# A decoder layer in three-product fp32: four of eight k pairs of the gate/up chunks in seven products, and an adding DMA for four additions

## The chip, the cores and the metric

The kernel runs on one core of a Trainium2 chip. The metric is the device time of one execution in microseconds (us). The engines are TensorE (PE; its weight loads are PEld), VectorE (DVE), ScalarE (ACT), GpSimd (POOL) and SyncE (SP); each takes its own instructions strictly in order, and an instruction that waits holds up all that stand behind it on its engine.

## The reference

One decoder layer on x of 256 x 2048 floats: an input projection that feeds a retention branch and a sliding-window attention branch, an output projection, and a SwiGLU feed-forward with d_ff = 5632. The change is in the feed-forward, with a small part at the very start (the first columns of the input projection).

```python
proj = h @ w_in[l]
...
h = layer_norm(DEEPNORM_ALPHA * h + merged @ w_out[l], ln1_g[l], ln1_b[l])
ffn = (jax.nn.silu(h @ w_gate[l]) * (h @ w_up[l])) @ w_down[l]
h = layer_norm(DEEPNORM_ALPHA * h + ffn, ln2_g[l], ln2_b[l])
```

## The kernel before

**Products.** Every fp32 product is made of three products of a shorter float type: high x high, high x low (the low part is that of the weights) and low x high. So each block of weights that a DMA brings on SP's queue (1 MB, tile `raw`) is split: ACT casts it to the high part (`wh`, L304 or L217), and DVE subtracts that from the block to get the low part (`wl`, L305 or L218). There are three buffers for `wh` and three for `wl` (pool `spl`). One matmul has 128 x 128 operands on one side and 512 columns on the other.

**Chunks.** The work is a stream of chunks. A gate/up chunk (f = 1 to 10) computes 512 columns of the gate and the same 512 of the up projection for both halves of the 256 rows, so it has four sums C11, C12, C21, C22, over 16 k tiles taken as eight pairs. An ordinary pair ("s") needs 8 products of a k tile with a half of the columns, 24 matmuls. Some pairs are computed in seven products in place of eight, by Winograd's form of Strassen's method ("S" pairs). An S pair is worked in two steps: step R (9 matmuls, into the sums P1, C11 and C12; cast `wh` of 1536 columns), and step T (12 matmuls, into P5, P7, P6 and C21), whose weights are differences of the blocks (`tsum`, three DVE instructions, L290 to L292) that are cast into `th` (ACT, L304) and `tl` (DVE, L305). There is one buffer for `th` and one for `tl` (pool `sp2`). `pair_seq(n)` gives the order of the pairs: S, s, S, s, ... until n S pairs are done, then the s pairs that are left. With n = 3 (NQ before) a gate/up chunk has three S and five s pairs, 183 matmuls, and its last three pairs are s pairs.

**Ends.** After the last T step, `mids` joins P1, P5, P6 and P7 into four partial results (one ACT copy of P1, L734, and four DVE additions). At the end of a chunk `done_gu` adds C11, C12, C21 and C22 to them (DVE), applies silu (ACT) and multiplies (DVE). Eight transposes on PE (L540) and a split into high and low parts (`ph`, `pl`, by ACT and DVE) make the left operand of the down projection of it. The sums of a chunk lie in banks of PSUM, eight in all; the first steps of the next chunk need banks that ACT's copy or DVE's additions have read out.

**Order.** The gate/up chunks stand in three parts, f = 0 to 3, 4 to 7 and 8 to 10 (f = 0 is a plain chunk), and each part is followed by its down-projection chunks, which are pair chunks as well: two after each of the first two parts, and one, with two plain chunks, after the last. NS is the number of S pairs in these. Left operands of S pairs are sums of the k tiles' parts (`hsums`, `psums`: small DVE additions and a split). Small background jobs are mixed in, two steps after each step of a chunk (`pump`). A list scheduler then lays out the instructions of each engine, so that the final order is not that of the code.

## Time and profile before

| | us |
|---|---|
| median of 3 runs (1432.46 to 1432.58) | 1432.5 |
| the profiled execution | 1432.52 |
| its span, first to last instruction | 1430.7 |
| PE busy | 1423.1 (99%) |
| DVE busy | 1135.0 (79%) |
| ACT busy | 699.3 (49%) |

The span is what the trace covers; 1.8 us of the profiled execution lie around it. A busy time is the time in which an engine had at least one instruction under way. Durations of neighbouring matmuls overlap, so the time that one costs is the distance of two starts, not its duration; the same holds on ACT and DVE, by less.

### The profile page before, as it was taken

The page shows a single profiled execution, that of the slowest core. Times are in us where ns is not written, and L with a number is a line of the kernel's source. Part 1 is how long each engine was busy: PE and PEld are TensorE (multiplying, and loading weights), DVE is VectorE, ACT ScalarE, POOL GpSimd, SP SyncE. Part 2 cuts the span into 40 slices and gives each one's busy share as a digit, 9 for nine tenths or more (in the row PEclk, how much of TensorE's full clock was granted, in tenths as well). Part 3 has the DMA queues.
Part 4 walks back from the last instruction along what each step waited for, and adds up shares of the span by engine and source line. Part 5 has one row for each costly group of instructions (what it writes and reads, how often), then busy time and mean ns, then how long its engine had stood idle before and what let it go on. Part 6 is the DMA issues. An engine that isn't in the chain of part 4 may idle for free.

```text
span 1430.7 us, 16141 instructions
## 1 busy us (share of the span) xinstructions
PE 1423.1 (99%) x6494; PEld 1165.0 (81%) x6494; DVE 1135.0 (79%) x1271; ACT 699.3 (49%) x664; POOL 0.9 (0%) x6
## 2 busy tenths in 40 slices
PE   9999999999999999999999999999999999999998
PEld 6878888878888878788888888888888888888886
DVE  6764555487878879776589989888999988898986
ACT  5465444344445445444345555445555455455542
...
GB/s 327 222 158 118 143 115 122 150 174 210 198 209 166 210 188 206 206 244 272 160 177 177 208 184 211 193 209 193 196 195 206 206 206 181 197 211 200 213 234 88
DMA packets 40235, 274.75 MB, mean 192 GB/s; under 512 B 4704, under 2 KB 4832, under 8 KB 8160
## 3 DMA queue, kind: packets, MB, share of 16 engines
...
## 4 chain that ended last, share of the span: by engine, by line
PE 98%; DVE 1%; DMA 0%; ACT 0%; SPq 0%; issue 0%
PE bank L324 21%; PE bank L326 21%; PE bank L325 21%; PE acc L235 9%; PE acc L233 9%; PE acc L234 9%; PE tr L540 2%; PE mx L589 2%; PE mx L618 1%; PE bank L540 1%; PE bank L235 1%; PE bank L234 1%; PE bank L233 1%; DMA xraw<-in_xw 0%; PE bank L685 0%; PE mx L656 0%
## 5 line engine op out<-in xcount | busy, mean ns | idle before, releaser
L304 ACT CAST wh<-raw 128x2048 fp32r<-128x2048 f32 (+1 forms) x174 | 307.7, 1769 | 295.1 <-PE bank L326 223.8
L305 DVE TENSOR_TENSOR wl<-raw,wh 128x2048 fp32r<-128x2048 f32 (+1 forms) x174 | 366.4, 2108 | 62.0 <-ACT wh L304 61.6
L218 DVE TENSOR_TENSOR wl<-raw,wh 128x2048 fp32r<-128x2048 f32 x70 | 160.1, 2288 | 79.6 <-ACT wh L217 79.3
L217 ACT CAST wh<-raw 128x2048 fp32r<-128x2048 f32 x70 | 133.5, 1909 | 175.0 <-PE acc L235 110.8
L324 PE MATMUL bank<-wh,hh 128*128 128x512 f32 x460 | 179.6, 390 | 0.0
L326 PE MATMUL bank<-wh,hl 128*128 128x512 f32 x460 | 179.1, 389 | 0.0
L325 PE MATMUL bank<-wl,hh 128*128 128x512 f32 x460 | 179.0, 389 | 0.0
L305 DVE TENSOR_TENSOR tl<-tsum,th 128x2048 fp32r<-128x2048 f32 x58 | 132.6, 2287 | 34.2 <-ACT th L304 34.0
L304 ACT CAST th<-tsum 128x2048 fp32r<-128x2048 f32 x58 | 111.0, 1914 | 95.1 <-DVE tsum L292 78.0
L324 PE MATMUL bank<-wh,xh 128*128 128x512 f32 x364 | 144.5, 397 | 0.0
L326 PE MATMUL bank<-wh,xl 128*128 128x512 f32 x364 | 141.8, 389 | 0.0
L325 PE MATMUL bank<-wl,xh 128*128 128x512 f32 x364 | 141.7, 389 | 0.0
L233 PE MATMUL acc<-wh,xh 128*128 128x512 f32 x352 | 140.9, 401 | 0.4 <-ACT wh L217 0.3
L235 PE MATMUL acc<-wh,xl 128*128 128x512 f32 x352 | 138.7, 394 | 0.0
L234 PE MATMUL acc<-wl,xh 128*128 128x512 f32 x352 | 138.0, 392 | 0.7 <-DVE wl L218 0.7
L326 PEld LDWEIGHTS bank<-wh,hl 128*128 128x128 f32 x460 | 86.3, 188 | 18.0
L325 PEld LDWEIGHTS bank<-wl,hh 128*128 128x128 f32 x460 | 86.4, 188 | 17.8
L324 PEld LDWEIGHTS bank<-wh,hh 128*128 128x128 f32 x460 | 86.4, 188 | 17.7
L324 PE MATMUL bank<-wh,ph 128*128 128x512 f32 x220 | 85.9, 390 | 0.0
L325 PE MATMUL bank<-wl,ph 128*128 128x512 f32 x220 | 85.6, 389 | 0.0
L326 PE MATMUL bank<-wh,pl 128*128 128x512 f32 x220 | 85.1, 389 | 0.0
L324 PEld LDWEIGHTS bank<-wh,xh 128*128 128x128 f32 x364 | 68.3, 188 | 15.8 <-issue 1.4
(287 smaller groups left out, 2315.2 us busy)
## 6 DMA issues: line engine op xcount, KB each, us to landing
raw<-in_w_gu SPq DMA_DIRECT2D x88, 1024.0 KB, 4.9
raw<-in_w_ip SPq DMA_DIRECT2D x56, 1024.0 KB, 4.9
raw<-in_w_in SPq DMA_DIRECT2D x40, 1024.0 KB, 4.9
raw<-in_w_dp SPq DMA_DIRECT2D x38, 1024.0 KB, 4.9
raw<-in_w_out SPq DMA_DIRECT2D x16, 1024.0 KB, 5.3
raw<-in_w_dl SPq DMA_DIRECT2D x6, 1024.0 KB, 4.9
...
hres<-in_x SPq DMA_DIRECT2D x1, 2048.0 KB, 7.9
```

The source lines that it names most:

```text
L217: nc.scalar.copy(out=h[:, 0:m], in_=r)
L218: nc.vector.tensor_sub(out=l[:, 0:m], in0=r, in1=h[:, 0:m].bitcast(F32))
L233: nc.tensor.matmul(self.acc[t], lhsT=xh, rhs=wh[:, j], start=st, stop=False)
L234: nc.tensor.matmul(self.acc[t], lhsT=xh, rhs=wl[:, j], start=False, stop=False)
L235: nc.tensor.matmul(self.acc[t], lhsT=xl, rhs=wh[:, j], start=False, stop=sp)
L304: nc.scalar.copy(out=h_, in_=r)
L305: nc.vector.tensor_sub(out=l_, in0=r, in1=h_.bitcast(F32))
L324: nc.tensor.matmul(self.acc[p], lhsT=xh, rhs=wh[:, j], start=st, stop=False)
L325: nc.tensor.matmul(self.acc[p], lhsT=xh, rhs=wl[:, j], start=False, stop=False)
L326: nc.tensor.matmul(self.acc[p], lhsT=xl, rhs=wh[:, j], start=False, stop=sp)
L540: m = nc.tensor.transpose(ps[:, i], s, ident)
L589: nc.tensor.matmul(sps[u][:, i], lhsT=qT[u * HD:(u + 1) * HD, h // 2], rhs=kT[u * HD:(u + 1) * HD, g, 0:W], start=True, stop=True)
```

## The change

It has five parts.

1. NQ goes from 3 to 4: four of the eight pairs of each gate/up chunk are S pairs, and the order of the pairs is S, s, S, s, S, s, S, s. NS goes from (3, 3, 2) to (3, 3, 3): one more S pair in the last down-projection pair chunk. On PE this takes away 33 matmuls of 512 columns (three in each of ten gate/up chunks, three in the last pair chunk). For each of these 11 new S pairs ACT has one cast of 2048 columns (`th`) more and one of the `wh` casts of 1536 in place of 2048; DVE has `tl` (2048), and `tsum` (one of 1024 and two of 512) more, and one `wl` of 1536 in place of 2048. There is one more `hsums` step before the gate/up chunks and one more `psums` step in the last part.
2. In seven of the ten gate/up chunks (f = 1, 2, 4, 5, 6, 8, 9) the four additions of `done_gu` go: ACT copies C11, C21, C12 and C22 from PSUM into the tile `cc` (four copies of 512 columns), and one DMA on POOL's queue adds the four tiles of `mids` (1 MB, SBUF to SBUF) onto it. A job `swish` applies silu (ACT, one instruction of 1024 columns) and multiplies (DVE, one of 1024) twelve and more job steps later, and the transposes wait for it. In f = 3, 7 and 10, the last of each part, DVE still adds, and all background jobs are run out first (`drain`).
3. The four tiles of `mids` become one tile `q4`; the scratch tiles of `hsums` are taken from the `tsum` buffer; the `psums` job pauses 14 (or 6) job steps after each pair.
4. The first chunk's blocks of x and weights are 1, 1, 1, 1 and six times 2 k tiles in place of 1, 1 and seven times 2, six buffers in place of four, with up to five blocks under way; the fourth warm-up matmul, of 256 columns, goes; the constants come in two DMAs on ACT's queue instead of one.
5. Some small tiles move to other pools (attention's in the pool `sma`, the sums of the left operand in the pool `hq`).

```diff
--- before.py
+++ after.py
@@ -28,7 +28,7 @@
 NWARM = 3
 TD = 14
 CP = 1
-NQ = 3
+NQ = 4
 NX = 2
 PG = 4
 NGEN = 3
@@ -334,7 +334,7 @@
                 self.done(self)
 
     LOOK_B = 3
-    XB = 4
+    XB = 6
 
     class Stream:
         def __init__(self):
@@ -354,7 +354,7 @@
         def ahead(self):
             while True:
                 cb = self.casts[min(self.ci, len(self.casts) - 1)][2]
-                while self.bi < min(len(self.blocks), cb + LOOK_B):
+                while self.bi < min(len(self.blocks), cb + (LOOK_B if cb >= len(XS) - LOOK_B else XB - 1)):
                     ch, b = self.blocks[self.bi]
                     ch.dma(b)
                     self.bi += 1
...
@@ -434,10 +435,8 @@
     for i in range(NWARM):
         wp = bank("tr", [P, C])
         nc.tensor.matmul(wp, lhsT=warm[:, 0:P], rhs=warm[:, P:P + C], start=True, stop=True)
-    wp = bank("tr", [P, C])
-    nc.tensor.matmul(wp[:, 0:SEQ], lhsT=warm[:, 0:P], rhs=warm[:, P:P + SEQ], start=True, stop=True)
-
-    XS = [1, 1, 2, 2, 2, 2, 2, 2, 2]
+
+    XS = [1, 1, 1, 1, 2, 2, 2, 2, 2, 2]
     xraw = {}
 
     def x_dma(b):
@@ -446,7 +445,8 @@
         nc.sync.dma_start(out=r[:, 0:XS[b]], in_=a["xw"][:, k:k + XS[b]])
         xraw[b] = r
         if b == 2:
-            nc.scalar.dma_start(out=cst[:, 0:NC0], in_=a["consts"][:, 0:NC0])
+            nc.scalar.dma_start(out=cst, in_=a["consts"][:, 0:P])
+            nc.scalar.dma_start(out=freq, in_=a["consts"][:, P:NC0])
             xraw["pos"] = xa.tile([P, LINE], I32, name="posi")[:, 0:2]
             nc.scalar.dma_start(out=xraw["pos"], in_=a["pos"])
 
...
@@ -727,16 +727,15 @@
 
     def mids(ch):
         tp, acc = sc["tp"], ch.acc
-        s1 = tp.tile([P, C], F32, name="s1")
-        vx = tp.tile([P, C], F32, name="vx")
-        w = tp.tile([P, C], F32, name="w")
-        x5 = tp.tile([P, C], F32, name="x5")
+        q = tp.tile([P, 4, C], F32, name="q4")
+        s1, vx, w, x5 = [q[:, i] for i in range(4)]
         nc.scalar.copy(out=s1, in_=acc["P1"])
         nc.vector.tensor_add(out=vx, in0=s1, in1=acc["P6"])
         nc.vector.tensor_add(out=w, in0=vx, in1=acc["P5"])
         nc.vector.tensor_add(out=vx, in0=vx, in1=acc["P7"])
         nc.vector.tensor_add(out=x5, in0=vx, in1=acc["P5"])
         ev["t"] = (s1, vx, w, x5)
+        ev["q"] = q
 
     def done_va(ch, j):
         acc = ch.acc
@@ -901,13 +900,13 @@
     sgf = {}
     ujobs = []
     parts = ((0, 4), (4, 8), (8, 11))
-    NS = (3, 3, 2)
+    NS = (3, 3, 3)
     f0_of = {f: f0 for f0, f1 in parts for f in range(f0, f1)}
     ND = {f: n for (f0, f1), n in zip(parts, NS) for f in range(f0, f1)}
 
     def done_g(ch, t, c):
         if t == 0:
-            sgf[c] = sc["fp"].tile([P, 2, C], F32, name="sg2", bufs=1)
+            sgf[c] = sc["fp"].tile([P, 4, C], F32, name="cc", bufs=1)
         nc.scalar.activation(out=sgf[c][:, t], in_=ch.acc[t], func=AF.Silu)
 
     def done_u(ch, t, c):
@@ -959,14 +958,16 @@
     def lhs_s(kp, i):
         return sc["sh"][:, i, kp], sc["sl"][:, i, kp]
 
-    def psums(ph, pl, k0, n):
-        yield
-        yield from hsums(ph, pl, sc["psh"], sc["psl"], n, k0)
+    def psums(ph, pl, k0, n, gap):
+        for _ in hsums(ph, pl, sc["psh"], sc["psl"], n, k0):
+            for _ in range(gap):
+                yield
 
     def hsums(hh, hl, sh, sl_, n, k0=0):
         for kp in range(n):
-            h2 = sc["tp"].tile([P, 2, 2, P], F32, name="s1")
-            sm = sc["tp"].tile([P, 4, P], F32, name="vx")
+            ts = sc["tp"].tile([P, 4, C], F32, name="tsum")
+            h2 = ts[:, 0].rearrange("p (k t c) -> p k t c", k=2, t=2)
+            sm = ts[:, 1].rearrange("p (k c) -> p k c", k=4)
             ks = slice(2 * kp, 2 * kp + 2)
             nc.vector.tensor_add(out=h2.rearrange("p k t c -> p k (t c)"), in0=hh[:, ks].bitcast(F32), in1=hl[:, ks].bitcast(F32))
             nc.vector.tensor_add(out=sm[:, 0], in0=h2[:, 0, 1], in1=h2[:, 1, 1])
@@ -982,31 +983,47 @@
 
     def flush():
         if "u" in ev:
-            f, args = ev.pop("u")
-            queue_p(f, [Job(u_bg(*arg)) for arg in args])
+            f, args, deps = ev.pop("u")
+            queue_p(f, [Job(u_bg(*arg), deps) for arg in args])
 
     def queue_p(f, js):
         kp = 2 * (f - f0_of[f])
         n = min(2, ND[f] - kp)
         if n > 0:
-            jobs["ps", f] = Job(psums(*pTs[f], kp, n), js)
+            jobs["ps", f] = Job(psums(*pTs[f], kp, n, 14 if f < 8 else 6), js)
 
     def done_gu(ch, f):
         acc = ch.acc
         s1, vx, w, x5 = ev["t"]
-        sg = sc["fp"].tile([P, 2, C], F32, name="sg2", bufs=1)
+        cc = sc["fp"].tile([P, 4, C], F32, name="cc", bufs=1)
         pTs[f] = (sc["pp"].tile([P, 4, SEQ], F32R, name="ph"), sc["pp"].tile([P, 4, SEQ], F32R, name="pl"))
-        nc.vector.tensor_add(out=sg[:, 0], in0=s1, in1=acc["C11"])
-        nc.scalar.activation(out=sg[:, 0], in_=sg[:, 0], func=AF.Silu)
+        us = [(cc, t, *pTs[f]) for t in range(2)]
+        if f + 1 not in (4, 8, 11):
+            for i, nm in enumerate(("C11", "C21", "C12", "C22")):
+                nc.scalar.copy(out=cc[:, i], in_=acc[nm])
+            nc.gpsimd.dma_start(out=cc, in_=ev["q"], accum_op=ALU.add)
+            ev["u"] = f, us, [Job(swish(cc))]
+            return
+        nc.vector.tensor_add(out=cc[:, 0], in0=s1, in1=acc["C11"])
+        nc.scalar.activation(out=cc[:, 0], in_=cc[:, 0], func=AF.Silu)
         nc.vector.tensor_add(out=w, in0=w, in1=acc["C12"])
-        nc.vector.tensor_add(out=sg[:, 1], in0=vx, in1=acc["C21"])
-        nc.scalar.activation(out=sg[:, 1], in_=sg[:, 1], func=AF.Silu)
-        nc.vector.tensor_mul(out=sg[:, 0], in0=sg[:, 0], in1=w)
+        nc.vector.tensor_add(out=cc[:, 1], in0=vx, in1=acc["C21"])
+        nc.scalar.activation(out=cc[:, 1], in_=cc[:, 1], func=AF.Silu)
+        nc.vector.tensor_mul(out=cc[:, 0], in0=cc[:, 0], in1=w)
         nc.vector.tensor_add(out=x5, in0=x5, in1=acc["C22"])
-        nc.vector.tensor_mul(out=sg[:, 1], in0=sg[:, 1], in1=x5)
-        ev["u"] = f, [(sg, t, *pTs[f]) for t in range(2)]
-        if f + 1 in (4, 8, 11):
-            flush()
+        nc.vector.tensor_mul(out=cc[:, 1], in0=cc[:, 1], in1=x5)
+        drain()
+        ev["u"] = f, us, []
+        flush()
+
+    def swish(cc):
+        for _ in range(12):
+            yield
+        tc.keep_in_program_order(nc.scalar.activation(out=cc[:, 0:2], in_=cc[:, 0:2], func=AF.Silu))
+        yield
+        yield
+        nc.vector.tensor_mul(out=cc[:, 0:2], in0=cc[:, 0:2], in1=cc[:, 2:4])
+        yield
 
     seq = pair_seq(NQ)
     for part, (f0, f1) in enumerate(parts):
...
-    sc["sh"] = hp.tile([P, 4, NQ, P], F32R, name="sh")
-    sc["sl"] = hp.tile([P, 4, NQ, P], F32R, name="sl")
...
+    hq = ppc.enter_context(tc.tile_pool(name="hq", bufs=1, side=RIGHT))
+    sc["sh"] = hq.tile([P, 4, NQ, P], F32R, name="sh")
+    sc["sl"] = hq.tile([P, 4, NQ, P], F32R, name="sl")
...
```

What it moves is shown at three places. A name's number tells one buffer's use from the next.

**ACT, the end of gate/up chunk f = 3 and the start of the down projection.** Before: the last T step's cast (`th_6305`), then the last two s pairs, and then the next chunk's first cast.

```order
L304 CAST wh_6311<-raw_6243 128x2048
L304 CAST th_6305<-tsum_6276 128x2048
L304 CAST wh_6341<-raw_6249 128x2048
L734 COPY s1_6374<-bank_6211 128x512
L304 CAST wh_6356<-raw_6309 128x2048
L304 CAST wh_6425<-raw_6315 128x1536
```

Now: `th_6299` is the third T step's cast, `wh_6406` and `wh_6443` are those of the next chunk's first R step and s pair, and `th_6366` is the cast of this chunk's fourth and last T step.

```order
L304 CAST wh_6372<-raw_6303 128x2048
L732 COPY q4_6431<-bank_6197 128x512
L304 CAST th_6299<-tsum_6270 128x2048
L304 CAST wh_6406<-raw_6309 128x1536
L304 CAST wh_6443<-raw_6370 128x2048
L304 CAST th_6366<-tsum_6336 128x2048
L400 CAST ph_6168<-bank_6484 128x4x128
L304 CAST wh_6502<-raw_6376 128x1536
```

The last T step's cast now stands behind two casts of the next chunk. `wh_6443` takes the buffer of `wh_6305`, and so waits for that pair's last matmul. On PE, at the same place, now:

```order
L324 MATMUL bank_6229<-wh_6305,hh_4751 128x512
L325 MATMUL bank_6229<-wl_6306,hh_4751 128x512
L326 MATMUL bank_6229<-wh_6305,hl_4752 128x512
L540 MATMUL bank_6484<-cst_80,cc_6167 128x128 [waits DMASW1_49]
L540 MATMUL bank_6484<-cst_80,cc_6167 128x128 x3
L324 MATMUL bank_6217<-th_6366,sh_5405 128x512 [waits Activation_49]
L324 MATMUL bank_6221<-th_6366,sh_5405 128x512
L324 MATMUL bank_6225<-th_6366,sh_5405 128x512
L324 MATMUL bank_6229<-th_6366,hh_4751 128x512
L325 MATMUL bank_6217<-tl_6367,sh_5405 128x512 [waits DVE_49]
L326 MATMUL bank_6217<-th_6366,sl_5406 128x512
```

Between the last matmul of `wh_6305` and the first of `th_6366` stand four transposes. The four products with `th_6366` are followed at once by those that need `tl_6367`, and what is left of the last s pair (six matmuls, into the bank that the T step's last sum also goes to) stands behind the T step.

**ACT, from gate/up chunk f = 5 to f = 6.** Before: `wh_7510` is the last s pair of f = 5, `wh_7579` the first R step of f = 6; the copy of P1 (L734) stands 6 rows ahead of the next chunk's s pair.

```order
L734 COPY s1_7528<-bank_7365 128x512
L304 CAST wh_7510<-raw_7463 128x2048
L304 CAST wh_7579<-raw_7469 128x1536
L401 CAST ph_7347<-bank_7561 128x4x128
L401 CAST ph_7347<-bank_7566 128x4x128
L304 CAST th_7583<-tsum_7575 128x2048
L304 CAST wh_7613<-raw_7499 128x2048
L1000 ACTIVATE sg2_7643<-sg2_7643 128x512
L304 CAST wh_7676<-raw_7514 128x1536
```

Now: `wh_7650` is the second R step of f = 6, `th_7588` its first T step, and the four copies (L1003) are those of f = 5.

```order
L304 CAST th_7517<-tsum_7487 128x2048
L732 COPY q4_7582<-bank_7356 128x512
L304 CAST wh_7594<-raw_7521 128x2048
L304 CAST wh_7650<-raw_7527 128x1536
L304 CAST th_7588<-tsum_7553 128x2048
L1003 COPY cc_7624<-bank_7360 128x512
L1003 COPY cc_7624<-bank_7380 128x512
L1003 COPY cc_7624<-bank_7364 128x512
L1003 COPY cc_7624<-bank_7399 128x512
```

The copies that free the sums' banks stand behind two casts, the first of which takes the buffer of the last s pair of f = 5 and so can't start before that chunk's last matmul. On PE, behind that matmul, now:

```order
L540 MATMUL bank_7637<-cst_80,cc_7340 128x128 x3
L324 MATMUL bank_7654<-wh_7557,hh_4751 128x512 [waits DVE_49]
L325 MATMUL bank_7654<-wl_7558,hh_4751 128x512
L326 MATMUL bank_7654<-wh_7557,hl_4752 128x512
L324 MATMUL bank_7654<-wh_7650,hh_4751 128x512 [waits Activation_49]
L325 MATMUL bank_7654<-wl_7651,hh_4751 128x512 [waits DVE_49]
L324 MATMUL bank_7658<-wh_7557,hh_4751 128x512 [waits Activation_49]
```

`bank_7658` is C11 of f = 6; it lies where `bank_7360`, C11 of f = 5, lay, which the first of the four copies reads out. Eight transposes and five matmuls stand between the chunk's last matmul and this one.

**DVE, from gate/up chunk f = 7 to the down projection.** Before: `mids` (L735 to L738) stands apart from the additions of `done_gu` (L999 to L1006). Of the latter:

```order
L305 TENSOR_TENSOR tl_8205<-tsum_8196,th_8204 128x2048
L290 TENSOR_TENSOR tsum_8275<-raw_8135 128x1024
L291 TENSOR_TENSOR tsum_8275<-raw_8135,tsum_8275 128x512
L305 TENSOR_TENSOR wl_8235<-raw_8120,wh_8234 128x2048
L999 TENSOR_TENSOR sg2_8264<-s1_8149,bank_7990 128x512
L1001 TENSOR_TENSOR w_8151<-w_8151,bank_7994 128x512
L1002 TENSOR_TENSOR sg2_8264<-vx_8150,bank_8010 128x512
L1004 TENSOR_TENSOR sg2_8264<-sg2_8264,w_8151 128x512
```

Now the two run into each other:

```order
L733 TENSOR_TENSOR q4_8202<-q4_8202,bank_7996 128x512
L291 TENSOR_TENSOR tsum_8173<-raw_8080,tsum_8173 128x512
L734 TENSOR_TENSOR q4_8202<-q4_8202,bank_7988 128x512
L292 TENSOR_TENSOR tsum_8173<-raw_8080,tsum_8173 128x512
L735 TENSOR_TENSOR q4_8202<-q4_8202,bank_7992 128x512
L1007 TENSOR_TENSOR cc_8244<-q4_8202,bank_7972 128x512
L736 TENSOR_TENSOR q4_8202<-q4_8202,bank_7988 128x512
L1009 TENSOR_TENSOR q4_8202<-q4_8202,bank_7976 128x512
L305 TENSOR_TENSOR tl_8209<-tsum_8173,th_8208 128x2048
L1010 TENSOR_TENSOR cc_8244<-q4_8202,bank_8000 128x512
L1012 TENSOR_TENSOR cc_8244<-cc_8244,q4_8202 128x512
L1013 TENSOR_TENSOR q4_8202<-q4_8202,bank_8019 128x512
```

The four additions of `mids` have moved to the chunk's end, in among those of `done_gu`; the products L1012 and L1014, which the eight transposes need, stand behind them and behind a `tl` of 2048 columns. The first sum of the down-projection chunk lies in the bank that L735 reads (`bank_7992`).

## Rows read from the trace of the kernel before

**Rows 1.** The page: busy time of the engines, share of the span, instructions.

```profile
PE 1423.1 (99%) x6494; PEld 1165.0 (81%) x6494; DVE 1135.0 (79%) x1271; ACT 699.3 (49%) x664; POOL 0.9 (0%) x6
```

**Rows 2.** The page: the chain that ended last, by engine.

```profile
PE 98%; DVE 1%; DMA 0%; ACT 0%; SPq 0%; issue 0%
```

**Rows 3.** Waits of PE: us in total, times, longest.

```profile
PE tr L436 <- POOL warm L432: 1.5, 1, 1.5
PE acc L234 <- DVE wl L218: 0.7, 2, 0.5
```

**Rows 4.** Windows of gate/up chunks: busy us (instructions) of PE, PEld, DVE, ACT, POOL.

```profile
1017.00:1060.00 43.00, 43.00 (x195) 35.71 (x194) 38.99 (x35) 21.96 (x16) 0.00 (x0) 1.00 0.54 195
1060.00:1102.50 42.50, 42.50 (x193) 35.25 (x192) 41.33 (x46) 22.99 (x18) 0.00 (x0) 1.00 0.56 198
```

**Rows 5.** Timeline of PE, f = 4: start, duration, instruction.

```profile
996.25 0.39 PE L326 MATMUL bank<-wh,hl 128*128 128x512 f32 x1
996.48 0.39 PE L324 MATMUL bank<-wh,hh 128*128 128x512 f32 x1
...
1000.11 0.39 PE L325 MATMUL bank<-wl,hh 128*128 128x512 f32 x1
1000.50 0.73 PE L324 MATMUL bank<-th,sh 128*128 128x512 f32 x2
```

**Rows 6.** Timeline of ACT at the same place.

```profile
996.72 1.91 ACT L304 CAST wh<-raw 128x2048 fp32r<-128x2048 f32 x1 [4.63 <-PE bank L326]
998.54 1.91 ACT L304 CAST th<-tsum 128x2048 fp32r<-128x2048 f32 x1
```

**Rows 7.** Timeline of DVE at the same place.

```profile
998.67 2.29 DVE L305 TENSOR_TENSOR wl<-raw,wh 128x2048 fp32r<-128x2048 f32 x1 [2.17 <-ACT wh L304]
1000.88 2.28 DVE L305 TENSOR_TENSOR tl<-tsum,th 128x2048 fp32r<-128x2048 f32 x1
```

**Rows 8.** Timeline of ACT at the end of f = 7.

```profile
1125.07 0.58 ACT L734 COPY s<-bank 128x512 f32<-128x512 f32 x1
...
1145.52 1.47 ACT L304 CAST wh<-raw 128x1536 fp32r<-128x1536 f32 x1
1146.90 0.62 ACT L1003 ACTIVATE sg<-sg 128x512 f32<-128x512 f32 x1
```

**Rows 9.** Timeline of PE at the end of f = 7.

```profile
1144.80 0.39 PE L326 MATMUL bank<-wh,hl 128*128 128x512 f32 x1
1145.03 0.39 PE L324 MATMUL bank<-wh,ph 128*128 128x512 f32 x1
...
1147.07 0.60 PE L540 MATMUL bank<-cst,sg 128*128 128x128 f32 x4
1147.42 0.47 PE L324 MATMUL bank<-wh,ph 128*128 128x512 f32 x1
```

**Rows 10.** Timeline of DVE at the end of f = 7.

```profile
1144.27 0.68 DVE L999 TENSOR_TENSOR sg<-s,bank 128x512 f32<-128x512 f32 x1
1144.87 0.68 DVE L1001 TENSOR_TENSOR w<-w,bank 128x512 f32<-128x512 f32 x1
...
1148.47 1.75 DVE L305 TENSOR_TENSOR wl<-raw,wh 128x1536 fp32r<-128x1536 f32 x1
1150.14 1.28 DVE L402 TENSOR_TENSOR pl<-bank,ph 128x512 fp32r<-128x512 f32 x2
```

**Rows 11.** Groups by form, DVE: busy us, mean ns of one, idle before.

```profile
L290 DVE TENSOR_TENSOR tsum<-raw 128x1024 f32<-128x1024 f32 x58 | 70.7, 1220 | 5.3 <-DMA raw<-in_w_gu 3.2 <-DMA raw<-in_w_ip 1.6
```

**Rows 12.** The page: DMA issues, KB each, us to landing.

```profile
raw<-in_w_gu SPq DMA_DIRECT2D x88, 1024.0 KB, 4.9
hres<-in_x SPq DMA_DIRECT2D x1, 2048.0 KB, 7.9
```

**Rows 13.** Timeline of the start, PE and ACT.

```profile
5.68 0.41 ACT L457 CAST xh<-xraw 128x256 fp32r<-128x256 f32 x1 [3.01 <-DMA xraw<-in_xw]
...
6.66 0.50 PE L233 MATMUL acc<-wh,xh 128*128 128x512 f32 x1 [0.28 <-ACT wh L217]
...
7.38 0.50 PE L234 MATMUL acc<-wl,xh 128*128 128x512 f32 x1 [0.22 <-DVE wl L218]
...
11.56 0.50 PE L234 MATMUL acc<-wl,xh 128*128 128x512 f32 x1 [0.53 <-DVE wl L218]
```

21 lines of the change are left out of this document (11 added, 10 removed).

## The prediction

> **What bounds the kernel now.** I read the page's busy times first, then the chain, then PE's waits, and only then single stretches. PE is busy for 1423.1 of 1430.7 us [rows 1], the chain that ended last is 98% PE [rows 2], and PE's waits together are about 2 us, all at the very start [rows 3]. So the time is the number of matmuls times their distance, and the reader should look for two things only: matmuls that go, and places where PE would begin to wait. Nine matmuls of 512 columns take from 1145.03 to 1147.07, 0.2267 us each, and four transposes 0.35 to 0.4 us [rows 9]. DVE, with 79% over the whole, is much fuller where the change works: in one gate/up window it is busy 41.33 of 42.50 us, in another 38.99 of 43.00 [rows 4]. PE doesn't wait there, because what it needs was made long before: the copy of P1, with which `mids` begins, starts 20 us ahead of the chunk's end (1125.07 against 1145.03) [rows 8, 9].
>
> **What the change takes off PE.** 33 matmuls by 0.2267 us are 7.5 us. At the start PE waits 0.28, 0.22 and 0.53 us for the first blocks [rows 13]; smaller blocks can give back at most this 1.0 us and the short warm-up matmul, and at least nothing, since the first cast at 5.68 us waits for a DMA that is as large as before. The second DMA for the constants is issued on ACT's queue, which waits for data until 5.68 us anyhow. I take 0.8. Without new waits the kernel would gain 8.3 us: 1432.5 - 8.3 = 1424.2.
>
> **What it puts on ACT and DVE.** On DVE a new S pair costs one `tl` of 2.21 us [rows 7], a `tsum` of 1.22 + 2 x 0.60 [rows 10, 11] and a `wl` of 1.67 in place of 2.21 [rows 7, 10]: about 4.1 us more. Seven chunks give back four additions and two products of 0.60 against one product of 1.22, 2.4 us. PE at the same time needs 0.7 us less a chunk. So a gate/up chunk in which DVE was busy 41.33 of 42.50 us [rows 4] wants about 43.0 in one of 41.8. The cover under which late low parts were caught up is gone, and the cost shows as waits at places that the order fixes. I work them out one by one.
>
> **The chain that prices them.** In f = 4 of before one such wait can be read whole. The last matmul of a pair ends its slot at 996.48; ACT, which waited for that pair's buffer, starts a cast 0.24 us later (996.72), the next cast, `th`, at 998.54, and PE's first product with `th` stands at 1000.50 [rows 5, 6]. So "pair ends, cast of 2048, cast of `th`, product" is 4.02 us. PE had 16 matmuls to fill it, and lost 0.16 us between 1000.11 and 1000.50. With a cast of 1536 in place of the first (1.38 us from its start to the next [rows 8], against 1.82) it is 3.58 us. DVE's `wl` starts 2.19 us after 996.48 and the next, `tl`, at 4.40, done at 6.65 [rows 5, 7].
>
> **First, the last T step of f = 3 and f = 2.** The order shows `th_6366` behind `wh_6406` and `wh_6443`, and the latter waits for the last matmul of `wh_6305`, behind which PE has only four transposes (0.4 us). The chain of 4.02 us leaves a wait of 3.6. Then come four products (0.9 us) to 4.93, and the `tl` isn't there before 6.65: 1.7 more. f = 2 has the same order with nine matmuls more (2.0 us): 1.6 + 1.7. Together 8.6 us. Lower bound: nothing, if ACT's wait were on another buffer; upper: 11, if DVE is late on top.
>
> **Second, the seams between chunks.** From f = 5 to 6 the first copy that frees a bank stands behind the casts `wh_7650` and `th_7588`. The first can't start before the chunk's last matmul: 0.24 + 1.38 + 1.82 + 0.58 for the copy [rows 8] + 0.05 to PE = 4.07 us. PE has eight transposes and five matmuls for it, 2.0 us; it waits 2.1. The seam from 9 to 10 has the same order: 2.1. From 6 to 7 only the 1536 cast and a copy of 0.5 stand ahead: 2.75 against 1.5, so 1.2. Where the copies come first (1 to 2, 4 to 5, 8 to 9) and from 2 to 3, I count 0.3 each. Sum 6.6, between 2 and 9.
>
> **Third, the three ends of parts** (f = 3, 7, 10), where DVE still adds. In before `mids` is done 20 us early and `done_gu` takes six rows of 0.60 us [rows 8, 10]. Now `mids` can't start before the T step's P6, which ends about 8 matmuls and four transposes, 2.2 us, ahead of the next chunk's first matmul; that waits for L735, the fifth of five rows: 0.24 + 5 x 0.60 = 3.25, a wait of 1.0 (2.5 if the `wl` ahead is still running). PE then has 24 matmuls, 5.4 us, and the first four transposes are just covered (L1007, L736, L1009, `tl`, L1010, L1012: 5.2). The second four need L1013, a `pl` and L1014, 1.8 us on: 1.2 of wait. The low part of the next R step stands behind another `pl`, a `tsum` and its own 1.67 us: 3.5 against 2.45 of PE's work, 1.0. That is 3.2, between 2 and 4.7; I take 3.0 for each, 9.0.
>
> **Fourth, inside the chunks.** In f = 4, 5, 8 and 9 the cast of the next R step, which waits for an s pair's last matmul, stands ahead of `th`: 3.58 us against 15 matmuls (3.40), 0.18 us each, some eight times more than before: 1.4.
>
> Sum: 8.6 + 6.6 + 9.0 + 1.4 = 25.6 us of new waits against 8.3 saved: 1432.5 + 17.3 = 1449.8, say 1450. The profiled execution (1432.52) is the median, so nothing is to be shifted.
>
> **The adding DMA.** No row of before shows one from SBUF to SBUF. Nearest: 1 MB from memory lands in 4.9 us, 2 MB in 7.9 [rows 12]. It is issued right behind the copies, and the silu that needs it stands on ACT behind the casts up to the third s pair, some 15 us on. At 5 to 10 us it costs nothing; each us beyond 15 holds ACT's casts in seven chunks. A rule speaks against it: the Trainium skill, "SBUF — State Buffer", "Summary: rules for kernel authors", says that a DMA issued from GpSimd isn't to be hidden under VectorE's work, since its descriptors are starved while VectorE runs in its fast modes. With DVE busy 97% of a window that would make the DMA wait for the gaps, and it is the last rival below. Its section "Who interferes with whom" takes tensor_tensor out of this, which is what all DVE's rows in these chunks are; no run here shows it yet.
>
> **Rivals.**
> - *PE hardly waits: 1422 to 1429.* ACT is busy only about half of the time [rows 4]. If its casts stand ready where I have them waiting for a buffer, the chains shorten to the `th` cast alone (0.24 + 1.91), and the waits stay under 5 us in all. For it: DVE at 97% cost PE nothing in before. Against: the one place in before with this order, 1000.50, shows just the wait that the chain gives. It ends on the other side once the waits fall below 8.3 - 2.9 = 5.4 us. Chance 0.14.
> - *Half of the waits.* If only the seams and the ends of parts come (15.6), or each wait is partly filled by work that the order shows behind it, the sum of waits is 6 to 16, and the time 1430 to 1440, around 1435. Chance 0.12, a little over half of it inside the band of no change.
> - *The adding DMA is late.* If it takes 20 us in place of under 15, the silu holds ACT's queue 5 us in each of seven chunks: 35 us, most of it PE's, about 1475. For it: DVE's fullness and the rule above; against: its own exception and the landing rows. Chance 0.06.
> - *My forecast:* 1440 to 1458, around 1450. Chance 0.68.
>
> **The numbers.** Changes within 0.2% (2.9 us) count as none. Faster has the first rival, 0.14; no change takes 0.07 of the second; slower has the rest, 0.79. The range runs from 1429, where the first rival ends, to 1459, where the upper bounds of the terms (11, 9 and 14, against 8.6, 6.6 and 9.0) would lie if nearly all of their excess came together; 0.14 lies below it and 0.06 above.
>
> **What would show it.** In the changed kernel's profile PE's waits for `th`, `tl` and banks should be a dozen microseconds or more, on L324 <- ACT `th` and L325 <- DVE `tl`, with gaps of 3 and 1.7 us in the last 30 matmuls of f = 3, and 2 us behind the transposes from f = 5 to 6 with ACT's L1003 as the releaser. Matmuls should keep 0.2267 us between gaps. Each transfer of the adding DMA should land in 5 to 10 us, and L1022 should wait for nothing. I am wrong if PE stays at 99% busy in the windows from 760 to 1360 us, or if the wait stands at L1022.

## The result, and the profile after

The changed kernel takes 1480.79 us (median of 4 runs, 1477.82 to 1485.0) against 1432.54 before: 1.0339 times as long, with a 95% interval of 1.0312 to 1.0366. The forecast was 1450, so the direction was right and the loss is 48.3 us where 17.3 were forecast. The profiled execution is the longest of the four (1485.0 us), with a span of 1483.2 us.

The page of the changed kernel, busy times, the chain that ended last, and the line of the adding DMA:

```profile
PE 1437.9 (97%) x6459; PEld 1160.5 (78%) x6459; DVE 1170.9 (79%) x1294; ACT 730.2 (49%) x700; POOL 7.0 (0%) x13
...
PE 77%; DVE 10%; DMA 5%; ACT 4%; issue 3%; SPq 0%; ACTq 0%; DVEq 0%
...
cc<-q POOLq DMA_DIRECT2D x7, 1024.0 KB, 8.0
```

PE is busy 14.8 us longer than before with fewer matmuls [rows 1], and the chain, 98% PE before [rows 2], is 77% PE now. In it stand DVE, DMAs and ACT. PE's waits in the changed kernel (us in total, times, longest):

```profile
PE bank L324 <- ACT th L304: 17.3, 11, 3.4
PE bank L324 <- DVE q L735: 4.2, 4, 1.7
PE bank L325 <- DVE wl L305: 3.3, 5, 1.1
PE bank L540 <- DVE cc L1014: 3.1, 3, 1.1
PE bank L325 <- DVE tl L305: 2.9, 2, 1.5
PE bank L540 <- DVE pl L401: 2.4, 1, 2.4
PE bank L540 <- DVE cc L1012: 1.8, 2, 1.6
```

They are the kinds of rows that were forecast (`th`, `tl`, banks, the products L1012 and L1014), and all are new against [rows 3]. The longest is at the end of f = 3. PE's timeline there (start, duration, instruction, idle time before it and what ended it):

```profile
897.91 0.60 PE L540 MATMUL bank<-cst,cc 128*128 128x128 f32 x4
901.86 0.97 PE L324 MATMUL bank<-th,sh 128*128 128x512 f32 x3 [3.35 <-ACT th L304]
902.66 0.59 PE L324 MATMUL bank<-th,hh 128*128 128x512 f32 x1
904.59 0.79 PE L325 MATMUL bank<-tl,sh 128*128 128x512 f32 x1 [1.34 <-DVE tl L305]
```

From the start of the four transposes, which is the end of the last matmul's slot, to the first product with `th` 3.95 us pass; the chain read off f = 4 of before gave 4.02. The idle times are 3.35 and 1.34 us, where waits of 3.6 and 1.7 were forecast. But an idle time is counted from the end of a duration, and a matmul's duration of 0.39 us lasts 0.16 beyond its slot of 0.2267, so each wait costs some 0.16 us more than it shows. By the starts these two waits are 3.95 less the 0.35 of the transposes, 3.6, and 904.59 less 902.66 and a slot, 1.7.

What was in no term is the clock. Windows of 2 us behind that place: PE's busy time, the granted clock, DMA share, GB/s.

```profile
900.00:902.00 2.00, 0.14 (x1) 1.00 0.79 324
902.00:904.00 2.00, 1.25 (x4) 0.67 0.80 213
904.00:906.00 2.00, 1.41 (x3) 0.50 0.91 381
906.00:908.00 2.00, 2.00 (x6) 0.50 0.21 86
908.00:910.00 2.00, 2.00 (x7) 0.62 0.00 0
910.00:912.00 2.00, 1.56 (x10) 1.00 0.46 66
```

At the start of the second wait the granted clock falls from 1.00 to 0.50, the 1.2 GHz level. By the windows' shares it stays there for some 7 us, the first 2 of them in the wait, and is then full again, at 2.4 GHz. At 0.50 six matmuls start in 2 us in place of nine. The same happens at the end of f = 2 (849 to 858 us). Windows of 20 us, by their clock, find four such places, the last of them on the border of two windows (columns as above):

```profile
840.00:860.00 20.00, 17.00 (x64) 0.83 0.59 206
...
900.00:920.00 20.00, 14.95 (x57) 0.83 0.43 153
...
1320.00:1340.00 20.00, 17.97 (x71) 0.91 0.56 211
...
1380.00:1400.00 20.00, 16.90 (x74) 0.94 0.47 172
1400.00:1420.00 20.00, 17.30 (x77) 0.97 0.51 197
```

The shortfalls (0.17, 0.17, 0.09, 0.06 and 0.03 of 20 us) add up to 10.4 us, which is the most that the clock can have cost, since PE was partly waiting at the time. The matmuls that start 0.43 us apart in these four stretches, 36 of them, took 7.2 us more than at 0.2267.

### The profile page after: what moved, and what is told of

Same layout as the page of the kernel before. It is cut to its first block, busy times and chain, and to the rows that moved or that the text cites. A ratio compares the mean times of both kernels' runs of the same rounds, so it can differ in the third digit from the quotient of the medians.

```text
span 1483.2 us, 16164 instructions
## 1 busy us (share of the span) xinstructions
PE 1437.9 (97%) x6459; PEld 1160.5 (78%) x6459; DVE 1170.9 (79%) x1294; ACT 730.2 (49%) x700; POOL 7.0 (0%) x13
## 4 chain that ended last, share of the span: by engine, by line
PE 77%; DVE 10%; DMA 5%; ACT 4%; issue 3%; SPq 0%; ACTq 0%; DVEq 0%
PE bank L325 15%; PE bank L324 15%; PE bank L326 15%; PE acc L233 8%; PE acc L235 8%; PE acc L234 8%; DMA raw<-in_w_gu 4%; DVE wl L305 4%; ACT wh L304 2%; ACT th L304 2%; PE tr L540 2%; PE mx L589 1%; PE mx L618 1%; DVE tl L305 1%; DVE tsum L290 1%
## 5 line engine op out<-in xcount | busy, mean ns | idle before, releaser
L305 DVE TENSOR_TENSOR wl<-raw,wh 128x2048 fp32r<-128x2048 f32 (+1 forms) x174 | 361.0, 2075 | 89.8 <-ACT wh L304 89.1
L305 DVE TENSOR_TENSOR tl<-tsum,th 128x2048 fp32r<-128x2048 f32 x69 | 157.8, 2288 | 26.5 <-ACT th L304 25.9
L304 ACT CAST th<-tsum 128x2048 fp32r<-128x2048 f32 x69 | 131.6, 1908 | 63.3 <-DVE tsum L292 60.0
L325 PE MATMUL bank<-wl,hh 128*128 128x512 f32 x400 | 157.3, 393 | 2.7 <-DVE wl L305 2.7
L324 PE MATMUL bank<-wh,hh 128*128 128x512 f32 x400 | 156.9, 395 | 3.0 <-DVE q L735 2.4
L326 PE MATMUL bank<-wh,hl 128*128 128x512 f32 x400 | 155.5, 392 | 0.0
L324 PE MATMUL bank<-wh,xh 128*128 128x512 f32 x364 | 144.5, 397 | 0.0
L324 PEld LDWEIGHTS bank<-wh,hh 128*128 128x128 f32 x400 | 75.8, 190 | 21.3 <-DVE q L735 3.1
L325 PEld LDWEIGHTS bank<-wl,hh 128*128 128x128 f32 x400 | 75.7, 189 | 20.3 <-DVE wl L305 4.6
L326 PEld LDWEIGHTS bank<-wh,hl 128*128 128x128 f32 x400 | 75.7, 189 | 15.9
L290 DVE TENSOR_TENSOR tsum<-raw 128x1024 f32<-128x1024 f32 x69 | 84.1, 1218 | 2.2 <-DMA raw<-in_w_ip 1.7
L324 PE MATMUL bank<-wh,ph 128*128 128x512 f32 x214 | 83.2, 392 | 2.2 <-DVE q L735 1.7
```

The lines of the kernel that those rows point to most:

```text
L290: nc.vector.tensor_sub(out=x[:, 0:2], in0=r[:, 0:1].broadcast_to([P, 2, C]), in1=r[:, 1:4:2])
L304: nc.scalar.copy(out=h_, in_=r)
L305: nc.vector.tensor_sub(out=l_, in0=r, in1=h_.bitcast(F32))
L324: nc.tensor.matmul(self.acc[p], lhsT=xh, rhs=wh[:, j], start=st, stop=False)
L325: nc.tensor.matmul(self.acc[p], lhsT=xh, rhs=wl[:, j], start=False, stop=False)
L326: nc.tensor.matmul(self.acc[p], lhsT=xl, rhs=wh[:, j], start=False, stop=sp)
```

## The experiments

What they tell apart, first: **theory A**, the fourth S pair loads DVE and makes the T steps late; **theory B**, the adding DMA collides with the weights' DMAs; **theory C**, the buffers that are now shared (the scratch of `hsums` and `psums` in the `tsum` buffer, the one tile q4) tie the steps together.

**1. Three S pairs again, all else as changed.**

```diff
-NQ = 4
+NQ = 3
```

> The changed kernel with three S pairs in place of four in each gate/up chunk, all else as changed (adding DMA, shared scratch, first chunk, three S pairs in the last down-projection pair chunk). Theory A (the fourth S pair makes DVE and the chunk's last T step late): the seven adding DMAs alone cost nothing, PE has 30 matmuls more than the changed kernel (6.8 us) and no waits of note: 1428 to 1434 us. Theory B (the adding DMA collides with the weights' DMAs, whose blocks then come late): the waits stay for the most part, 1455 to 1475 us. Theory C (the scratch that hsums and the tsum share, and the one buffer of q4, tie the steps together): 1440 to 1455 us.

1434.57 us, 1.0013 times before (1.0004 to 1.0022), 0.6 above A's band. With three S pairs the rest of the change costs little: against the kernel of experiment 13 that has the start and the third S pair of the last pair chunk as well (1430.55), the adding DMA, the shared scratch, the one tile q4 and the pauses cost 4.0 us together; one wait of 2.2 us of L324 for a `pl` is left. That B and C could need the fourth pair was not foreseen in their expectations, so this run alone refutes neither.

**2. No adding DMA: DVE adds in all ten chunks.**

```diff
-        if f + 1 not in (4, 8, 11):
+        if False:
...
```

> The changed kernel without the adding DMA: in all ten gate/up chunks DVE makes the additions, as it does in f = 3, 7 and 10. Theory A: DVE has 2.4 us more in seven chunks, so the waits grow: 1482 to 1500 us. Theory B: without the DMA the weights' blocks come in time, 1435 to 1450 us. Theory C: as the changed kernel, 1470 to 1490 us.

1487.74 us, 1.0383 (1.0368 to 1.0399), in A's band, and in the upper end of C's. The adding DMA is worth 6.9 us to the changed kernel: it takes work off DVE. Theory B, which wanted 1435 to 1450 us, falls as the main cause.

**3. The adding DMA left out, with nothing in its place.**

```diff
-            nc.gpsimd.dma_start(out=cc, in_=ev["q"], accum_op=ALU.add)
```

> The changed kernel with the seven adding DMAs left out, and nothing in their place: the four partial sums of mids are not added in f = 1, 2, 4, 5, 6, 8 and 9. Theory A: the DMA was hidden, so within 4 us of the changed kernel, 1475 to 1484 us. Theory B: 1435 to 1455 us, and the weights' blocks of 1 MB land in under 6 us in every chunk. Theory C: as theory A.

1475.66 us, 1.031 (1.0292 to 1.0327), 5.1 us under the changed kernel, a little more than A's 4. Of four runs each the ranges still touch (1472.06 to 1479.19 against 1477.82 to 1485.0), so the size is rough, but the transfer isn't free. One place of the changed kernel shows how. ACT, DVE and PE between 1049 and 1068 us (chunk f = 5), behind an adding DMA that was issued at 1045.31:

```profile
1058.07 1.91 ACT L304 CAST wh<-raw 128x2048 fp32r<-128x2048 f32 x1 [3.96 <-DMA raw<-in_w_gu]
```

```profile
1060.01 2.29 DVE L305 TENSOR_TENSOR wl<-raw,wh 128x2048 fp32r<-128x2048 f32 x1 [3.58 <-ACT wh L304]
```

```profile
1067.94 0.96 PE L324 MATMUL bank<-th,sh 128*128 128x512 f32 x3 [3.28 <-ACT th L304]
```

The DMA issues of the same stretch, 1040 to 1072 us (KB each, median us to landing):

```profile
raw<-in_w_gu SPq DMA_DIRECT2D x5, 1024.0 KB, 7.6
cc<-q POOLq DMA_DIRECT2D x1, 1024.0 KB, 10.5
```

The weights' blocks land in 7.6 us there, and in 4.9 over the whole, as before [rows 12]; without the adding DMA they land in 4.8 in the same stretch. ACT waits 3.96 us for one, DVE 3.58 for ACT, and eight us later PE waits 3.28 for the `th` that comes behind. The adding DMA itself is in time: no row shows L1022 waiting.

**4. The kernel before with the fourth S pair alone.**

```diff
-NQ = 3
+NQ = 4
...
+    hq = ppc.enter_context(tc.tile_pool(name="hq", bufs=1, side=RIGHT))
+    sc["sh"] = hq.tile([P, 4, NQ, P], F32R, name="sh")
...
```

> The kernel before with the fourth S pair alone (and the sums of the left operand in a pool of their own, so that they fit): DVE's additions, scratch tiles apart, first chunk as before. Theory A: the fourth S pair brings the loss by itself, 1470 to 1500 us. Theory B: about the saving, 1425 to 1440 us. Theory C: 1430 to 1445 us.

1455.13 us, 1.016 (1.0145 to 1.0175), between all the bands: 22.6 us slower, 25.7 faster than the changed kernel. PE's waits there:

```profile
PE bank L324 <- ACT th L304: 4.7, 6, 0.9
PE bank L324 <- DVE sg L999: 3.9, 4, 1.1
PE bank L325 <- DVE wl L305: 2.0, 4, 0.8
PE bank L540 <- DVE sg L1004: 1.7, 1, 1.7
```

So the fourth pair is one half of the loss, though it saves 30 matmuls (6.8 us), and the other half is something else that the change brought with it.

**5. The same, with the scratch of `hsums` and `psums` in the `tsum` buffer.** Theory C is now told apart in three: C1 the `tsum` buffer, C2 the one tile q4, C3 the pauses of `psums`.

```diff
-            h2 = sc["tp"].tile([P, 2, 2, P], F32, name="s1")
-            sm = sc["tp"].tile([P, 4, P], F32, name="vx")
+            ts = sc["tp"].tile([P, 4, C], F32, name="tsum")
+            h2 = ts[:, 0].rearrange("p (k t c) -> p k t c", k=2, t=2)
+            sm = ts[:, 1].rearrange("p (k c) -> p k c", k=4)
```

> The kernel before with the fourth S pair (1455.1 us), and with the scratch of hsums and psums taken from the one tsum buffer, as in the changed kernel, in place of two of the mids tiles. Theory C1 (a psums step holds the tsum buffer while it waits for ACT, and the next T step's differences wait behind it): 1470 to 1490 us. Theory C2 (the one tile q4 of mids is what is freed late): 1452 to 1458 us. Theory C3 (the pauses of psums push its work into places where DVE is late): 1452 to 1458 us.

1486.92 us, 1.0379 (1.0363 to 1.0394): 31.8 us more than without it, in C1's band. Some of it is the clock: its mean is 0.995 in this run and 1.000 in experiment 4. DVE's timeline shows what the buffer does (from one `tl` to the next S pair's differences):

```profile
1099.14 2.29 DVE L305 TENSOR_TENSOR tl<-tsum,th 128x2048 fp32r<-128x2048 f32 x1 [0.37 <-ACT th L304]
1101.46 0.69 DVE L972 TENSOR_TENSOR tsum<-ph,pl 128x512 f32<-128x512 f32 x1
...
1106.41 0.69 DVE L972 TENSOR_TENSOR tsum<-ph,pl 128x512 f32<-128x512 f32 x1
...
1110.39 0.69 DVE L402 TENSOR_TENSOR psl<-tsum,psh 128x512 fp32r<-128x512 f32 x1 [0.69 <-ACT psh L401]
1111.12 1.23 DVE L290 TENSOR_TENSOR tsum<-raw 128x1024 f32<-128x1024 f32 x1
```

Two `psums` steps hold the one `tsum` buffer from 1101.46 to 1111.1; only then, 9.7 us after the last `tl` has let the buffer go, do the next S pair's differences begin, of which the next `th` and `tl` are made.

**6. The changed kernel with that scratch in the q4 buffer.**

```diff
-            ts = sc["tp"].tile([P, 4, C], F32, name="tsum")
+            ts = sc["tp"].tile([P, 4, C], F32, name="q4")
```

> The changed kernel (1480.8 us) with the scratch of hsums and psums taken from the q4 buffer in place of the tsum buffer. Theory C1: 1450 to 1465 us. Theory C2: the q4 buffer gets one more user, 1478 to 1500 us. Theory C3: as the changed kernel, 1475 to 1485 us.

1467.08 us, 1.0239 (1.0224 to 1.0255), 13.7 us under the changed kernel: the right way for C1, but not as far as its 1450 to 1465: the scratch now waits for q4, 8.5 us in all at L972, until the adding DMA has read it. No run has the changed kernel with this scratch in tiles of its own.

**7. The pauses of `psums` cut to one step.**

```diff
-            jobs["ps", f] = Job(psums(*pTs[f], kp, n, 14 if f < 8 else 6), js)
+            jobs["ps", f] = Job(psums(*pTs[f], kp, n, 1), js)
```

> The changed kernel with a pause of one job step in place of 14 or 6 after each pair of psums. Theory C1: the psums steps still take the tsum buffer, only earlier, 1472 to 1490 us. Theory C2: 1475 to 1485 us. Theory C3: 1455 to 1465 us.

1489.73 us, 1.0403 (1.0387 to 1.0418). The pauses help by 8.9 us; C3 falls.

**8. The kernel of experiment 4 with q4 as one tile, the scratch in it.**

```diff
+        q = tp.tile([P, 4, C], F32, name="q4")
+        s1, vx, w, x5 = [q[:, i] for i in range(4)]
...
```

> The kernel before with the fourth S pair (1455.1 us), and with the four tiles of mids as one tile with one buffer, from which hsums takes its scratch too. Theory C1: 1452 to 1460 us. Theory C2: 1470 to 1490 us. Theory C3: 1452 to 1460 us.

1462.08 us, 1.0215 (1.0198 to 1.0232): 7 us for the tile with the scratch in it, outside both bands, the smaller part.

**9. Where the S pairs stand.** What is left is the fourth pair's own 22.6 us. **Theory D**: DVE has too much to do; **theory E**: the last T step stands too late in the chunk.

```diff
+        if n == 4:
+            return [("S", 0), ("s", 4), ("S", 1), ("S", 2), ("s", 5), ("S", 3), ("s", 6), ("s", 7)]
```

> The kernel before with the fourth S pair (1455.1 us), with the pairs in the order S, s, S, S, s, S, s, s in place of S, s, S, s, S, s, S, s, so that two s pairs (48 matmuls, 10.9 us) stand behind the last T step. Theory D (DVE has too much to do in each chunk, wherever the S pairs stand): 1452 to 1465 us, two S pairs in a row make it no better. Theory E (the last T step stands at the chunk's end, so that mids, the additions and the next chunk's banks come late): 1430 to 1442 us.

1464.89 us, 1.0221 (1.0207 to 1.0235), 9.8 us worse than S and s in turn, where E wanted 1430 to 1442. That speaks against E as the main cause, though this order also sets two S pairs in a row, which by D is harder on DVE.

**10. Less work on DVE for each T step.** It leaves out two of the four differences.

```diff
+            if u == "T" and sc.get("light"):
+                nc.scalar.copy(out=h_, in_=r[:, 0:1].broadcast_to([P, 4, C]))
+                nc.vector.tensor_sub(out=l_[:, 0:2], in0=r[:, 0:2], in1=h_[:, 0:2].bitcast(F32))
...
```

> The kernel before with the fourth S pair (1455.1 us), where in the feed-forward DVE makes only two of an S pair's four difference blocks and their low parts, which are then used twice; ACT's cast of 2048 columns and PE's products stay as many. It leaves out two of the four differences. DVE has 2.3 us less for each S pair. Theory D: 1426 to 1436 us. Theory E: the last T step stands where it stood, 1443 to 1453 us.

1425.2 us, 0.9949 (0.9936 to 0.9963), 7.3 us faster than before: this kernel, with two S pairs in the last pair chunk, has 30 matmuls fewer, which are 6.8 us. No wait of PE for a T step is left. That is D's side (just under its band) and not E's. But the edit changes more than DVE's load, as the next experiment shows.

**11. The same edit in the changed kernel.** Its other half, which experiment 10 has too:

```diff
-                nc.vector.tensor_sub(out=x[:, 2], in0=r[:, 1], in1=x[:, 1])
-                nc.vector.tensor_sub(out=x[:, 3], in0=r[:, 2], in1=x[:, 2])
+                if not sc.get("light"):
+                    nc.vector.tensor_sub(out=x[:, 2], in0=r[:, 1], in1=x[:, 1])
+                    nc.vector.tensor_sub(out=x[:, 3], in0=r[:, 2], in1=x[:, 2])
```

> The changed kernel (1480.8 us), where in the feed-forward DVE makes only two of an S pair's four difference blocks and their low parts, which are used twice; it leaves out two of the four differences. Scratch shared, adding DMA, late last T step: all as changed. Theory D (all of the loss, that of the shared scratch and the clock's too, comes through DVE's lateness): 1422 to 1428 us. Rival (the shared scratch or the late T step costs by its order, even where DVE has time): 1435 to 1465 us.

1423.74 us, 0.9938 (0.9923 to 0.9953). So all 57 us between it and the changed kernel hang on what DVE does for the T steps, the loss by the shared scratch and by the clock with it. Its waits of PE that are not at the start:

```profile
PE bank L331 <- DVE tl L307: 0.8, 1, 0.8
...
PE bank L330 <- ACT th L306: 0.5, 1, 0.5
```

Windows of 1060 to 1200 us, busy times of PE, PEld, DVE, ACT and POOL, first of before, then of the changed kernel, then of this one:

```profile
1060.00:1200.00 140.00, 140.00 (x631) 116.03 (x630) 127.78 (x126) 73.65 (x55) 0.00 (x0) 1.00 0.55 194
```

```profile
1060.00:1200.00 140.00, 128.26 (x563) 101.78 (x562) 130.18 (x121) 77.80 (x63) 1.72 (x2) 1.00 0.58 195
```

```profile
1060.00:1200.00 140.00, 140.00 (x631) 115.92 (x630) 112.95 (x105) 80.88 (x60) 0.86 (x1) 1.00 0.65 218
```

DVE's busy share doesn't tell the first two apart: 128 and 130 of 140 us, and in the whole span 79% in both. Its work for one instruction of PE does. PE does 631 instructions in 140 us in before and here, and 563 in the changed kernel; at the pace of before these 563 would take 125 us (an estimate from the two counts), and DVE works 130 us for them. In experiment 4's kernel, in the same way, it is 137 us of DVE for 591 instructions, 131 us of PE. Over 760 to 1370 us the changed kernel's DVE has 535 us for 2492 instructions, 557 us at that pace: it is over the mark only in part of the stretch.

What this edit doesn't tell apart is how DVE's work costs. It cuts the load, and it also cuts an estimated 2.3 us from the chain of every T step (two subtractions of 0.60 and half of `tl`), and it moves `th` on ACT. ACT's timeline, first of the changed kernel, then of this one:

```profile
1050.82 1.48 ACT L304 CAST wh<-raw 128x1536 fp32r<-128x1536 f32 x1 [4.80 <-PE bank L326]
1052.21 1.90 ACT L304 CAST th<-tsum 128x2048 fp32r<-128x2048 f32 x1
```

```profile
1133.10 1.92 ACT L306 CAST th<-tsum 128x2048 fp32r<-128x2048 f32 x1 [0.85 <-PE bank L332]
1138.50 1.49 ACT L310 CAST wh<-raw 128x1536 fp32r<-128x1536 f32 x1 [3.48 <-PE bank L332]
```

In the changed kernel `th` stands right behind the next R step's cast, which here waits 4.80 us for PE, in 26 of 55 T steps from 760 us on, and in experiment 4's in 31 of 53; with this edit in 2 of 55, and in experiment 10 in none. So load, length of the chain and order change together.

**12. DVE's work moved to GpSimd.** Nothing is left out here; first the two subtractions of 512 columns, then all three of the differences.

```diff
-                nc.vector.tensor_sub(out=x[:, 2], in0=r[:, 1], in1=x[:, 1])
-                nc.vector.tensor_sub(out=x[:, 3], in0=r[:, 2], in1=x[:, 2])
+                nc.gpsimd.tensor_sub(out=x[:, 2], in0=r[:, 1], in1=x[:, 1])
+                nc.gpsimd.tensor_sub(out=x[:, 3], in0=r[:, 2], in1=x[:, 2])
```

> The kernel before with the fourth S pair and the changed start, and with the two subtractions of 512 columns of each S pair's differences on GpSimd in place of DVE; nothing is left out. DVE has 1.2 us less for each S pair. Theory D: about half of the loss goes, 1430 to 1445 us, if GpSimd takes no more than some 2 us for each. Rival (GpSimd is so slow, or holds up DVE so much, that the differences come late): 1455 to 1500 us.

> As the run before, with all three subtractions of the differences on GpSimd; nothing is left out. DVE has 2.4 us less for each S pair, as much as in the run with half of the differences (1425.2 us). Theory D: 1423 to 1430 us, if GpSimd isn't late. Rival (GpSimd's own time, three instructions for each S pair every ten us, becomes the bound): 1450 to 1550 us.

1531.0 us, 1.0681 (1.0667 to 1.0696), and 1550.72 us, 1.0826 (1.0812 to 1.0841). The groups of the first, GpSimd's and DVE's (busy us, mean ns of one, idle before):

```profile
L292 POOL TENSOR_TENSOR tsum<-raw,tsum 128x512 f32<-128x512 f32 x68 | 153.7, 2260 | 5.3
```

```profile
L305 DVE TENSOR_TENSOR wl<-raw,wh 128x2048 fp32r<-128x2048 f32 x106 | 281.7, 2662 | 50.9 <-ACT wh L304 50.8
```

Both are on the rival's side and above its bands. GpSimd takes 2.26 us for what DVE does in 0.69, twice in each T step's chain, and DVE's own `wl` goes from 2.29 [rows 7] to 2.66 us. In the first of the two `th` stands behind the next R step's cast in only 2 of 53 T steps, and DVE has less to do for PE than in experiment 4 (between 760 and 1370 us 498 us for 2348 instructions, against 571 for 2612), and still it is 76 us slower than that kernel: a longer chain costs by itself, with no more load on DVE.

**13. The start alone, and the start with three S pairs in the last pair chunk** (NS in the second kernel only).

```diff
-    XS = [1, 1, 2, 2, 2, 2, 2, 2, 2]
+    XS = [1, 1, 1, 1, 2, 2, 2, 2, 2, 2]
...
-NS = (3, 3, 2)
+NS = (3, 3, 3)
...
```

> The kernel before with the first chunk's blocks, buffers and look-ahead of the changed kernel, and without the fourth warm-up matmul; one DMA for the constants as before. My forecast's term: 0.8 us less than before, 1431.3 to 1432.0 us. Rival: the wait only moves to the next blocks, 1432.3 to 1432.8 us.

> The kernel before with the changed start (1430.6 us) and with three S pairs in place of two in the last down-projection pair chunk: three matmuls fewer, 0.7 us. If that chunk's six pairs leave DVE time: 1429.7 to 1430.1 us; if the new T step or psums comes late there: 1431 to 1434 us.

1430.58 us, 0.9986 (0.9977 to 0.9995), and 1430.55 us, 0.9986 (0.9977 to 0.9995). The start gives 1.9 us, more than my 0.8; the extra S pair gives nothing that can be told. These two, equal within the noise, are the fastest kernels of the study that leave nothing out.

**14. The start, and the fourth S pair in f = 4 and 8 alone.**

```diff
-                stream.add(PairChunk([a["w_gu"][f - 1, kp] for kp in range(KT // 2)], seq, lhs_h, lhs_s, mid_gu,
+                stream.add(PairChunk([a["w_gu"][f - 1, kp] for kp in range(KT // 2)], pair_seq(4 if f in (4, 8) else 3), lhs_h, lhs_s, mid_gu,
...
```

> The kernel before with the changed start and the fourth S pair in f = 4 and f = 8 alone, the first chunks after a down projection, where DVE has no psums and PE lost least in the run with the fourth S pair everywhere. Six matmuls fewer (1.4 us) and the start's 0.8: 1430 to 1431.5 us, if the lateness comes from DVE's load and stays within these chunks (theory D); 1432 to 1436 us, if the late T step costs at the seam wherever it stands (theory E).

1436.68 us, 1.0029 (1.0017 to 1.004), 6.1 us behind the start alone, above both bands and nearer to E's (1432 to 1436) than to D's. Two chunks with a fourth pair already cost more than they save (1.4 us). PE's waits for `th` and `pl` in that trace are 2.6 us; much of the rest lies in starts that no wait counts: ten first products with `th` start 0.33 to 0.48 us behind the matmul ahead of them, in the start alone four, and the next matmul follows after 0.34 in place of 0.2267. At such a place in f = 4 DVE isn't the one that is late; it waits for ACT, whose cast for the next R step stands ahead of `th` and waits for PE:

```profile
1007.04 1.76 DVE L305 TENSOR_TENSOR wl<-raw,wh 128x1536 fp32r<-128x1536 f32 x1 [1.62 <-ACT wh L304]
```

So a part of what the fourth pair costs comes from ACT's order, as the forecast's chains of 0.18 us have it, and not from DVE's load. How the 22.6 us of experiment 4 divide between the two stays open.

## Why the forecast failed in size, step by step

- **What bounds the kernel now**, and **what the change takes off PE**: right. With DVE's work for the T steps cut the changed kernel takes 1423.74 us, and the forecast without new waits was 1424.2. The start was mis-sized (1.9 for 0.8), and the extra S pair in the last pair chunk, 0.7 us by the sum, gave nothing (experiment 13).
- **The chain that prices the waits**: right, in the mechanism and in size. ACT's cast at 898.11 us waits for the last matmul, `th` stands behind it, and by the starts the waits at the end of f = 2 are 1.6 and 1.7 us, at f = 3 3.6 and 1.7: 8.6 us for the 8.6 of the first term. (PE's cover in the chain of before is 17 matmuls and not 16; nothing hangs on it.)
- **The seams**: too high, and for another reason than the text gave. Idle 0.98 + 0.47 us from f = 5 to 6 and 0.78 + 0.56 from 9 to 10 for 2.1 each, 0.66 from 6 to 7 for 1.2. What PE waits for is not ACT's copies (L1003), which the forecast named as the releaser, but DVE: the bank that the next chunk's P1 takes, which L735 has to read out first, and then a `wl`.
- **The ends of parts**: about right in sum. From f = 3 on, idle times of 0.44, 0.27 and 1.14; from f = 7 on, 0.44, 1.74, 0.81 and 0.67; at the last, 1.56 and 1.15. With 0.16 each that is 9.7 us for 9.0.
- **Inside the chunks** is the step that failed. I gave it 1.4 us, as chains of 0.18 that start with every engine on time. Chains of this size did come: 17 first products with `th` start 0.33 to 0.48 us behind the matmul ahead of them, 2.9 us beyond the slots (before: three, 0.5 us). But between 769 and 1335 us PE also idles 0.51 to 3.28 us at ten places inside the chunks, 13.5 us together, and twice more, 2.37 and 0.73, in f = 10; with 0.16 each, 18.5 us. Three of them, from PE's timeline of the changed kernel:

```profile
829.80 0.96 PE L324 MATMUL bank<-th,sh 128*128 128x512 f32 x3 [0.83 <-ACT th L304]
...
1149.06 0.97 PE L324 MATMUL bank<-th,sh 128*128 128x512 f32 x3 [1.92 <-ACT th L304]
...
1334.66 0.96 PE L324 MATMUL bank<-th,sh 128*128 128x512 f32 x3 [2.00 <-ACT th L304]
```

  The chain that ended last leads from each of them back through a block of weights. Its DMA could start only when DVE had let its buffer go, by a `wl` or the last of the three `tsum` instructions, and then it landed beside an adding DMA (the DMAs in that chain: start, duration):

```profile
815.94 10.02 DMA raw<-in_w_gu
...
1137.57 7.79 DMA raw<-in_w_gu
...
1317.21 7.49 DMA raw<-in_w_gu
```

  So what DVE does late comes back to PE some ten us and more later, by way of the block's buffer, the DMA, ACT's cast and `th`. (Without the adding DMA all but 5.1 us of the loss stays, so the slow landing itself is a small part.) That DVE wanted "about 43.0 in one of 41.8" stood in the text, and I took it as a cover that was gone, not as a lag that later chains start with. Experiment 11's window bears this out in part (130 us of DVE's work for 125 of PE's); how much is load, how much the chain's length and how much ACT's order isn't shown.
- **The edit that I left out of the sum** is the shared scratch, the third part of the change. It costs 31.8 us on top of the fourth pair in the kernel before (experiment 5), at most 4.0 with three pairs, together with the rest of the change (experiment 1), and nothing that shows with DVE's work for the T steps cut (experiment 11). In the changed kernel itself only the move to q4 was run, 13.7 us. A `psums` step in the `tsum` buffer had to be priced as a wait for that buffer, with the next T step behind it.
- **The clock** was in no term: 7.2 to 10.4 us in the profiled execution, each time right behind one or two waits, one of them of 1.3 us or more. In sum, waits and late starts are some 44 us where 25.6 were forecast, and the clock comes on top; a part of what is still missing is the first matmul behind each wait, 0.34 us in place of 0.2267.
- **The adding DMA**: "at 5 to 10 us it costs nothing" is wrong by some 5 us (experiment 3). It lands in 7.1 to 10.5 us, before the silu needs it, but the weights' blocks that share the time with it come late. It is still worth more than it costs: 6.9 us net against DVE's additions. The rule of the Trainium skill's page "SBUF — State Buffer" on DMAs from GpSimd, which I had as a rival, didn't bite here: all seven transfers land within 10.5 us, two of them in the window in which DVE is busy 130 of 140 us, as the exception for tensor_tensor in its section "Who interferes with whom" lets one expect. No run has the same transfer beside an idle DVE, so a smaller delay isn't excluded. The same section says that a VectorE instruction with both inputs in SBUF contends with GpSimd instructions that read SBUF; experiment 12 agrees (2.29 to 2.66 us).

The rivals: "half of the waits" and "PE hardly waits" are out. "The adding DMA is late" gave 1475 us, near the time, for a reason that experiments 2 and 3 refute: that it came near is luck.
